# Other places for the steps of an iteration in a chunked RWKV-7 recurrence, and the turned blocks fetched first

## The chip, the cores and the metric
The kernel runs on one core of a Trainium2 chip. The metric is the device time of one execution in microseconds; of the kernel before, three executions were timed. Profiles are taken from one further execution each. TensorE does matmuls, VectorE and ScalarE elementwise work, GpSimd some elementwise work, and SyncE issues the transfers (DMAs) between DRAM and the on-chip memory SBUF. TensorE writes to PSUM, which VectorE and ScalarE read.

## The reference
One layer of a diffusion backbone on 512 latent and 256 context tokens of width 1024: a half-step SwiGLU, then a mixer with two branches (RWKV-7 and RG-LRU, both scanned forwards and backwards, the latent scans starting from the final context states), then another SwiGLU. The change lies in the RWKV-7 scan, for 16 heads of size 64 and both directions:

```
def rwkv_step(s, inp):
    r, w, k, v, kk, kka = inp
    sa = einsum('bhvk,bhk->bhv', s, -kk)
    s = s * w[:, :, None, :] + sa[..., None] * kka[:, :, None, :] + v[..., None] * k[:, :, None, :]
    y = einsum('bhvk,bhk->bhv', s, r)
    return s, y
...
ys, finals = [], []
for d in (forward, backward):
    y, s_fin = rwkv_scan(r, w[d], k[d], v, kk, kk * a[d], s0[d], reverse=d == 1)
```

## The kernel before
The token axis is cut into 12 chunks of 64 tokens (4 of context, 8 latent), and inside a chunk the scan becomes matrix products. A **unit** is a pair of heads in one direction, so there are 16 units (0 to 15; even ones forwards, odd ones backwards). For each unit the kernel does, in this order:

- `loads`: brings features `bk` (b and k), `ar` (a and r) and decays `pc` from DRAM.
- `gram`: products of a and r with b (three operations: context, two halves of the latent chunks) and with k (two). ScalarE copies or VectorE masks them into the tile `gm` (lines 775, 776, 790, 791 and 793). PSUM buffers for these and other side products are called `wk`; there are three of them.
- `out`: the products with b go to DRAM (`nd`, four transfers, line 806) and come back in another layout (`wl`, two, line 810).
- `invert`: VectorE inverts 48 triangular blocks of 32 x 32 (two for each chunk and head) by 31 steps of a multiply (line 826) and a subtraction (line 828) on the tile `yl`. At the end (`end`) GpSimd copies the result turned into `ylt` (line 836), and both go to DRAM as `yd` (line 838) and `yt` (line 840), two transfers each.
- `back`: SyncE fetches the inverses as diagonal blocks into the tile `ybd` (Y in the code, four transfers, line 850), and the turned ones into `y1` (two, line 853). The profile drops the last digit of names, so it prints `y1` as `y`; `y<-yt` is the transfer into y1.
- `merge`: two rounds of 48 small matmuls build the off-diagonal blocks: the first reads `y1` (line 866), the second `ybd` (line 880). ScalarE copies each round's result.
- `fetch`: the decay matrices `dg` (GpSimd, line 897), and turned keys and values.
- `chain`: the serial part, 12 chunks of four steps each (`right`, `solve`, `step`, and reads of the output). ScalarE copies what each gives to the next.
- `finish`: for a pair of units, normalisation, in four operations (`load`, `mean`, `var`, `scale`); it runs in every second iteration.

Besides, a filler puts products of the other branch (tiles `fl`, `fx`, `fraw`) between the chain's steps, where TensorE would wait for ScalarE.

An **iteration** is 24 steps (12 chunks of half a chain) long. In iteration i the chains of units i and i+1 run side by side, four steps a chunk, and the other work belongs to units further ahead: `gram` and the start of `invert` to unit i+3, the end of `invert`, `back` and `merge` to unit i+2. A written table, WIN, says at which step of an iteration each operation stands; the numbers above 24 reach into the next iteration. All operations are sorted by these numbers, and each engine, SyncE's transfers too, gets its instructions in exactly this order, without any rearranging. Units 0 and 1 are inverted in a prologue beside other work. Iteration -1 is the first, with one chain only; iteration 13 is the first without `gram`.

```
                    put(i, zip(WIN["gram"], ops))
                    put(i, [(WIN["out"], out)])
                    put(i, [(WIN["inv"][0] - 0.5, unit_invert(i + 3, WIN["back"], WIN["inv"]))])
                ...
                    put(i, zip(WIN["mrg"], merge(i + 2)))
```

The operations of an inversion (a beginning, 31 steps, `end`) are spread evenly over the stretch WIN["inv"].

Of the kernel before, what the change touches and what calls it, by code (L numbers as in the profile page):

```python
# [8 lines left out]
F32 = mybir.dt.float32  # L9
# [18 lines left out]
NCH = NT // C  # L28
# [28 lines left out]
def hybrid_layer_kernel(ctx: ExitStack, tc, xT, vecs, cst_in, w_mod, wg1, wu1, wd1, w_in, w_up, a_up, g_up,  # L57
                        w_prw, lru_wa, lru_wx, w_plru, w_out, wg2, wu2, wd2, out):
    nc = tc.nc
# [641 lines left out]
    def rwkv_phase(outer, dense_in):  # L701
        with ExitStack() as st:
            open_psum(st, "ps_rwkv")
            units = ExitStack()
            up = units.enter_context(tc.tile_pool(name="units", bufs=1, reuse_waits="tile"))
# [47 lines left out]
            def each_head(out, lhsT, rhs, start=True, stop=True):  # L753

                for h in range(2):
                    PE.matmul(out[hp[h]], lhsT=lhsT[hp[h]], rhs=rhs[hp[h]], start=start, stop=stop)  # L756
# [57 lines left out]
            def invert(i):  # L814
                u = us[i]

                def begin():
                    u["yl"] = up.tile([96, 16, 32], F32, tag="yl", name="yl", bufs=2)
                    V.tensor_copy(u["yl"].rearrange("p i t -> p (i t)"), eye[:96])

                def step(t):
                    def go():
                        yl, wl = u["yl"], u["wl"]
                        ni, nt = t // 2 + 1, 31 - t
                        pr = up.tile([96, 16, 32], F32, tag="pr", name="pr", bufs=1)
                        V.tensor_tensor(out=pr[:, :ni, :nt], in0=yl[:, :ni, t:t + 1].to_broadcast([96, ni, nt]),  # L826
                                        in1=wl[:, t:t + 1, t + 1:].to_broadcast([96, ni, nt]), op=ALU.mult)
                        V.tensor_tensor(out=yl[:, :ni, t + 1:], in0=yl[:, :ni, t + 1:], in1=pr[:, :ni, :nt], op=ALU.subtract)  # L828
                    return go

                def end():
                    yl = u["yl"]
                    yd = dram.tile([48, 32, 32], F32, tag="yd", name="yd", bufs=3)
                    yt = dram.tile([24, 32, 2, 16], F32, tag="yt", name="yt", bufs=3)
                    ylt = up.tile([96, 32, 16], F32, tag="ylt", name="ylt", bufs=1)
                    G.tensor_copy(ylt, yl.rearrange("p i t -> p t i"))
                    for q in range(2):
                        nc.sync.dma_start(out=yd.rearrange("m (i q) t -> m i q t", q=2)[:, :, q, :], in_=yl[48 * q:48 * q + 48])
                    for q in range(2):
                        nc.sync.dma_start(out=yt[:, :, q, :], in_=ylt[48 * q:48 * q + 24])  # L840
                    u["yd"], u["yt"] = yd, yt

                def back():
                    yd, yt = u["yd"], u["yt"]
                    Y = u["Y"] = ybd[i % 3]
                    for b in range(2):
                        for h in range(2):
                            p0 = 64 * h + 32 * b
                            m0 = 24 * b + 12 * h
                            nc.sync.dma_start(out=Y[p0:p0 + 32, :, 32 * b:32 * b + 32], in_=yd[m0:m0 + 12].rearrange("m s t -> s m t"))  # L850
                    u["y1"] = up.tile([128, NCH, 32], F32, tag="y1", name="y1", bufs=1)
                    for h in range(2):
                        nc.sync.dma_start(out=u["y1"][64 * h:64 * h + 32],
                                          in_=yt[12 * h:12 * h + 12].rearrange("m t q i -> t m (q i)"))
                return [begin] + [step(t) for t in range(31)] + [end], back

            def merge(i):
                u = us[i]

                def first():  # L860
                    acc = work()
                    u["mid"] = up.tile([128, NCH * 32], F32, tag="mid", name="mid", bufs=1)
                    for c in range(NCH):
                        for h in range(2):
                            lo, hi = 64 * h, 64 * h + 32
                            PE.matmul(acc[hi:hi + 32, 32 * c:32 * c + 32], lhsT=u["n"][lo:lo + 32, c, 32:64],  # L866
                                      rhs=u["y1"][lo:lo + 32, c, :].rearrange("p (q i) -> p i q", q=2),
                                      start=True, stop=True, tile_position=(lo, hi))
                    for h in range(2):
                        hi = 64 * h + 32  # L870
                        S.activation(u["mid"][hi:hi + 32, :], acc[hi:hi + 32, :NCH * 32], AF.Copy)

                def second():
                    Y = u["Y"]
                    m3 = u["mid"].rearrange("p (c s) -> p c s", s=32)
                    acc = work()
                    for c in range(NCH):
                        for h in range(2):
                            lo, hi = 64 * h, 64 * h + 32
                            PE.matmul(acc[lo:lo + 32, 32 * c:32 * c + 32], lhsT=m3[hi:hi + 32, c, :],  # L880
                                      rhs=Y[hi:hi + 32, c, 32:64], start=True, stop=True, tile_position=(hi, lo))
                    for h in range(2):
                        lo = 64 * h
                        S.activation(Y[lo:lo + 32, :, 32:64],
                                     acc[lo:lo + 32, :NCH * 32].rearrange("p (c s) -> p c s", s=32), AF.Copy)

                return [first, second]
# [35 lines left out]
            def chain(i):  # L923
# [8 lines left out]
                def copied(src, tag):  # L932
                    t = up.tile([128, C], F32, tag=f"{tag}{d}", name=tag, bufs=2)
                    S.activation(t, src, AF.Copy)
                    return t
# [24 lines left out]
                def solve(pos):  # L960
                    def go():
                        c = seq[pos]
                        acc = u["chb"][:, 2 * C:3 * C]
                        each_head(acc, u["Y"][:, c], u["w"])
                        u["u"] = copied(acc, "u")
# [180 lines left out]
            def put(i, ops):  # L1146

                for a, op in ops:
                    at = HOPS * i + a

                    def go(at=at, op=op):
                        with tc.high_priority(tc.cur_priority - base - int(100 * (at + 3 * HOPS))):
                            op()
                    serial[0] += 1
                    todo.append((at, serial[0], go))
# [13 lines left out]
            def unit_invert(i, at, window):  # L1169
                def go():  # L1170
                    ops, back = invert(i)
                    put(i - 3, spread(ops, *window))
                    put(i - 3, [(at, back)])
                return go

            def iteration(i):
# [3 lines left out]
                if i >= 1 and i % 2 == 0:  # L1180
                    put(i, zip(WIN["fin"], finish(i // 2 - 1)))
                if 0 <= i + 4 < NU:
                    put(i, [(9.1, op) for op in loads(i + 4)])
                if 1 < i + 3 < NU:
                    ops, out = gram(i + 3)
# [3 lines that stand above are left out]
                if 1 < i + 2 < NU:  # L1189
                    put(i, zip(WIN["mrg"], merge(i + 2)))  # L1190
                if 0 < i + 2 < NU:
                    put(i, zip(WIN["tm"], fetch(i + 2)))
                if i < NU:
# [9 lines left out]
            def prologue():  # L1203
# [45 lines left out]
                for op in fetch(0):  # L1249
                    op()  # L1250


            WIN = dict(fin=(0.6, 4.6, 8.6, 16.6), gram=(0.7, 3.4, 4.7, 16.7, 20.7), out=5.0, inv=(11.0, 32.0), back=34.0,
                       mrg=(19.4, 22.0), tm=(0.3, 7.4, 8.7, 11.4, 12.7, 15.4), fill=(2.0, 10.0, 18.0), more=(2.0, 6.0, 10.0, 14.0, 18.0, 22.0))
            ALL = {mybir.EngineType.PE, mybir.EngineType.DVE, mybir.EngineType.Activation, mybir.EngineType.Pool, mybir.EngineType.SP}
            PREF = 50000
            SHARE = [6] * 14 + [16] * 3
# [1 line left out]
            with tc.manual_schedule(engines=ALL):  # L1259
                prologue()  # L1260
                fill = filler()
                for i in range(-1, NU):
                    iteration(i)
            with tc.manual_schedule(engines={mybir.EngineType.PE}):
                units.close()
                m = merge_phase(outer)
# [123 lines left out]
    with ExitStack() as outer:  # L1390
        dense_in = outer.enter_context(ExitStack())
        open_hn(dense_in, NT, "right")
        wpool = dense_in.enter_context(tc.tile_pool(name="weights", bufs=1, reuse_waits="tile", side="right"))
        WB = (3, 6, 6)
        ffn1_phase()
        input_phase()
        rwkv_phase(outer, dense_in)
# [67 lines left out]
```

## Time and profile before
| | us |
|---|---|
| median of three executions | 2440.74 |
| lowest and highest | 2434.94 and 2446.79 |
| the profiled execution | 2444.58 |
| its span, from the first to the last instruction | 2442.8 |
| TensorE busy | 2165.1 (89% of the span) |
| VectorE busy | 1320.9 (54%) |
| ScalarE busy | 928.9 (38%) |
| GpSimd busy | 326.0 (13%) |

Outside of the span lie 1.8 us. The recurrence takes the stretch from about 1345 to 1915 us of the span. The busy shares are means over very different stages, so they say nothing of what a place in the recurrence waits for; that is read from the chain of waits and from the order of times on each engine.

### The profile page before, as it was taken

Reading aid. Unit: us, or ns where it says so; the run is one execution under the profiler, and the core shown is the slowest. Engines: PE = TensorE matmul, PEld = TensorE weight load, DVE = VectorE, ACT = ScalarE, POOL = GpSimd, SP = SyncE. Lnnn points to the kernel's source line nnn. Section 1 sums busy time; section 2 is a strip of 40 time slices with the busy share of each in tenths; the row PEclk is TensorE's granted clock in tenths of the full one; section 3 lists DMA queues with packets and bytes.
Section 4 is the critical chain, followed back from the end, with each engine's and each line's share of the span. In section 5 each row is a group of like instructions: output and inputs, shape, how many; then the busy total and the mean of one; then the engine's idle time right before and its main releaser. Section 6 shows DMA issues by size and latency. Waiting matters only on the chain.

```text
span 2442.8 us, 49727 instructions
## 1 busy us (share of the span) xinstructions
PE 2165.1 (89%) x20408; PEld 1826.9 (75%) x20416; DVE 1320.9 (54%) x2795; ACT 928.9 (38%) x1977; POOL 326.0 (13%) x272
## 2 busy tenths in 40 slices
PE   5999999999697988969889788888888698999997
PEld 3788878788685767757667777787787478888886
DVE  5333223233876877778746466667672266333335
ACT  5322212213554556546632333334343235222223
POOL 1000000000352434324100111111111001000000
PEclk8999999999898989989999899999899798999999
DMA  7524342222436564564684445544542442333233
GB/s 290 195 58 147 114 160 70 91 65 74 130 97 112 120 105 116 119 85 127 104 220 137 121 111 128 135 98 126 133 109 76 158 155 87 91 103 99 83 95 91
DMA packets 254662, 289.15 MB, mean 118 GB/s; under 512 B 153953, under 2 KB 172641, under 8 KB 250209
## 3 DMA queue, kind: packets, MB, share of 16 engines
q1 hardware_dynamic: 254144, 285.37, 43.8%
q8 instruction: 160, 2.62, 0.5%
q10 hardware_dynamic: 288, 0.59, 0.1%
q14 instruction: 70, 0.57, 0.1%
HBM read 229.96 MB, written 55.93 MB: 117 GB/s over the span
## 4 chain that ended last, share of the span: by engine, by line
PE 36%; DMA 7%; DVE 4%; issue 2%; ACT 2%; SPq 2%; POOL 0%; DVEq 0%; POOLq 0%; ACTq 0%
PE mm L197 6%; PE mm L198 6%; PE mm L199 6%; PE ch L756 5%; PE wk L756 5%; DMA y<-yt 3%; PE y L957 1%; SPq L850 1%; DVE pr L826 1%; DVE yl L828 1%; PE wk L866 1%; PE fl L1089 1%; DMA ga_d<-sh 1%; DMA wraw<-in_w_in_dram 1%; PE wk L880 1%
## 5 line engine op out<-in xcount | busy, mean ns | idle before, releaser
L197 PE MATMUL mm<-hnh,whi 128*128 128x512 f32 (+1 forms) x1768 | 621.7, 353 | 29.3 <-ACT gr L475 22.3
L198 PE MATMUL mm<-hnl,whi 128*128 128x512 f32 (+1 forms) x1768 | 620.4, 351 | 2.5 <-POOL hnl L203 1.7
L199 PE MATMUL mm<-hnh,wlo 128*128 128x512 f32 (+1 forms) x1768 | 616.6, 349 | 0.0
L161 ACT ACTIVATE whi<-wraw 128x512 fp32r<-128x512 f32 (+3 forms) x264 | 193.5, 735 | 583.7 <-PE mm L198 467.4
L197 PEld LDWEIGHTS mm<-hnh,whi 128*128 128x128 f32 x1768 | 340.8, 193 | 90.6 <-issue 40.2
L179 DVE TENSOR_TENSOR wlo<-wraw,whi 128x512 fp32r<-128x512 f32 (+3 forms) x264 | 216.0, 820 | 316.7 <-ACT whi L161 313.3
L198 PEld LDWEIGHTS mm<-hnl,whi 128*128 128x128 f32 x1768 | 341.3, 193 | 53.2 <-issue 7.4
L199 PEld LDWEIGHTS mm<-hnh,wlo 128*128 128x128 f32 x1768 | 341.1, 193 | 42.5
L197 PE MATMUL mm<-hh,whi 128*128 128x256 f32 (+1 forms) x592 | 201.0, 340 | 0.5 <-ACT hh L202 0.5
L198 PE MATMUL mm<-hl,whi 128*128 128x256 f32 (+1 forms) x592 | 200.6, 339 | 0.3 <-DVE hl L203 0.3
L199 PE MATMUL mm<-hh,wlo 128*128 128x256 f32 (+1 forms) x592 | 200.5, 339 | 0.0
L826 DVE TENSOR_TENSOR pr<-yl,wl 96x126 f32<-96x126 f32 (+22 forms) x496 | 145.9, 294 | 46.2 <-DMA wl<-nd 32.4
L319 DVE TENSOR_TENSOR hf<-mm,sl 128x256 f32<-128x256 f32 (+1 forms) x68 | 40.1, 590 | 209.8 <-PE mm L199 207.9
L828 DVE TENSOR_TENSOR yl<-yl,pr 96x126 f32<-96x126 f32 (+22 forms) x496 | 134.3, 271 | 17.1
L179 POOL TENSOR_TENSOR wlo<-wraw,whi 128x512 fp32r<-128x512 f32 x86 | 134.8, 1568 | 6.1
L203 POOL TENSOR_TENSOR hnl<-nt,hnh 128x256 fp32r<-128x256 f32 (+1 forms) x28 | 27.1, 967 | 783.5 <-ACT hnh L202 649.4
L197 PEld LDWEIGHTS mm<-hh,whi 128*128 128x128 f32 x592 | 112.7, 190 | 15.2 <-issue 1.7
L199 PEld LDWEIGHTS mm<-hh,wlo 128*128 128x128 f32 x592 | 112.6, 190 | 15.2 <-issue 2.5
L198 PEld LDWEIGHTS mm<-hl,whi 128*128 128x128 f32 x592 | 112.6, 190 | 14.1 <-issue 0.8
L161 POOL CAST whi<-wraw 128x512 fp32r<-128x512 f32 x86 | 78.2, 910 | 301.3 <-PE mm L198 223.2
L343 DVE SCALAR_TENSOR_TENSOR res<-mm,scl,res 128x256 f32<-128x256 f32 (+1 forms) x112 | 66.9, 597 | 92.5 <-PE mm L199 91.5
L756 PE MATMUL wk<-ar,bk 64*64 64x128 f32 (+1 forms) x1536 | 95.3, 273 | 2.9 <-DMA ar<-ar_d 2.9
(268 smaller groups left out, 3726.2 us busy)
## 6 DMA issues: line engine op xcount, KB each, us to landing
wm<-in_w_mod_dram SPq DMA_DIRECT2D x32, 1024.0 KB, 5.5
wraw<-in_w_in_dram SPq DMA_DIRECT2D x118, 256.0 KB, 5.8
wraw<-in_wd_dram SPq DMA_DIRECT2D x64, 256.0 KB, 2.8
bk_d<-bk SPq DMA_DIRECT2D x16, 768.0 KB, 13.3
bk<-bk_d SPq DMA_DIRECT2D x16, 768.0 KB, 5.8
wraw<-in_wg_dram SPq DMA_DIRECT2D x44, 256.0 KB, 2.7
wraw<-in_wu_dram SPq DMA_DIRECT2D x44, 256.0 KB
wraw<-in_wg_dram SPq DMA_DIRECT2D x22, 512.0 KB
```

What stands on the lines that cost most here:

```text
L161: self.copy = (lambda o, i: eng.tensor_copy(o, i)) if eng else (lambda o, i: S.activation(o, i, AF.Copy))
L179: self.sub.tensor_tensor(out=l[:, :m], in0=raw[:, :m], in1=h[:, :m], op=ALU.subtract)
L197: PE.matmul(acc, lhsT=wh, rhs=xh, start=k == 0, stop=False)
L198: PE.matmul(acc, lhsT=wh, rhs=xl, start=False, stop=False)
L199: cur["pe"] = PE.matmul(acc, lhsT=wl, rhs=xh, start=False, stop=k == n - 1).ins.name
L203: eng.tensor_tensor(out=lo, in0=src, in1=hi, op=ALU.subtract)
L319: V.tensor_tensor(out=hf[:, :n], in0=pu[:, :n], in1=sl[:, :n], op=ALU.mult)
L343: V.scalar_tensor_tensor(out=res[:, m, q:q + n], in0=acc[:, :n], scalar=scl[:, gi, m, v:v + 1], in1=res[:, m, q:q + n], op0=ALU.mult, op1= ...
L756: PE.matmul(out[hp[h]], lhsT=lhsT[hp[h]], rhs=rhs[hp[h]], start=start, stop=stop)
L826: V.tensor_tensor(out=pr[:, :ni, :nt], in0=yl[:, :ni, t:t + 1].to_broadcast([96, ni, nt]), in1=wl[:, t:t + 1, t + 1:].to_broadcast([96, ni ...
L828: V.tensor_tensor(out=yl[:, :ni, t + 1:], in0=yl[:, :ni, t + 1:], in1=pr[:, :ni, :nt], op=ALU.subtract)
L850: nc.sync.dma_start(out=Y[p0:p0 + 32, :, 32 * b:32 * b + 32], in_=yd[m0:m0 + 12].rearrange("m s t -> s m t"))
```

## The change
Two things change in `invert`, and the table gets other numbers.

- `end`: yd and yt of each half are issued in turn (yd, yt, yd, yt) instead of both yd and then both yt. Both transfers wait for what they read: yd for `yl`, yt for the turned copy.
- `back`: y1 is fetched before `ybd`, and of `ybd` the blocks b = 1, which the second merge reads, first.
- The table: the products with b move from steps 0.7, 3.4, 4.7 to 0.7, 2.0, 3.4; `out` from 5.0 to 3.6; the inversion from 11.0 to 32.0 to 9.5 to 28.0; `back` from 34.0 to 29.5; `merge` from 19.4 and 22.0 to 22.1 and 23.4; the second product with k from 20.7 to 19.4; the filler's first place from 2.0 to 6.0.

```
                     for q in range(2):
                         nc.sync.dma_start(out=yd.rearrange("m (i q) t -> m i q t", q=2)[:, :, q, :], in_=yl[48 * q:48 * q + 48])
-                    for q in range(2):
                         nc.sync.dma_start(out=yt[:, :, q, :], in_=ylt[48 * q:48 * q + 24])
...
                 def back():
                     yd, yt = u["yd"], u["yt"]
+                    u["y1"] = up.tile([128, NCH, 32], F32, tag="y1", name="y1", bufs=1)
+                    for h in range(2):
+                        nc.sync.dma_start(out=u["y1"][64 * h:64 * h + 32],
+                                          in_=yt[12 * h:12 * h + 12].rearrange("m t q i -> t m (q i)"))
                     Y = u["Y"] = ybd[i % 3]
-                    for b in range(2):
+                    for b in (1, 0):
                         for h in range(2):
...
-            WIN = dict(fin=(0.6, 4.6, 8.6, 16.6), gram=(0.7, 3.4, 4.7, 16.7, 20.7), out=5.0, inv=(11.0, 32.0), back=34.0,
-                       mrg=(19.4, 22.0), ...
+            WIN = dict(fin=(0.6, 4.7, 8.6, 16.6), gram=(0.7, 2.0, 3.4, 16.7, 19.4), out=3.6, inv=(9.5, 28.0), back=29.5,
+                       mrg=(22.1, 23.4), ...
```

The order of SyncE's transfers in one iteration with `finish`, before (y_14775 is y1 of this unit, ybd_10268 its Y):

```order
L895 DMA vs<-zv_d 128x768
L1097 DMA plru_d<-sg 128x256
L806 DMA nd<-gm 32x12x32 x4
L810 DMA wl<-nd 48x1024 x2
L838 DMA yd<-yl 768x1x32 x2
L840 DMA yt<-ylt 768x1x16 x2
L1018 DMA fa<-ga_d 128x512
L1019 DMA fa<-gb_d 128x512
L741 DMA bk<-bk_d 128x1536
L743 DMA ar<-ar_d 128x1280
L747 DMA pc<-pc_d 128x12
L850 DMA ybd_10268<-yd 32x12x32 x4
L853 DMA y_14775<-yt 32x12x32 x2
```

The same place in the changed kernel:

```order
L895 DMA vs<-zv_d 128x768
L838 DMA yd<-yl 768x1x32
L839 DMA yt<-ylt 768x1x16
L838 DMA yd<-yl 768x1x32
L839 DMA yt<-ylt 768x1x16
L806 DMA nd<-gm 32x12x32 x4
L810 DMA wl<-nd 48x1024 x2
L846 DMA y_14660<-yt 32x12x32 x2
L853 DMA ybd_10268<-yd 32x12x32 x4
L1097 DMA plru_d<-sg 128x256
L1018 DMA fa<-ga_d 128x512
L1019 DMA fa<-gb_d 128x512
```

yd and yt, which belong to the unit before, now stand ahead of nd and wl, and y1 stands right behind wl.

VectorE at the end of an inversion (of the changed kernel; the last two operations of a step of `yl` end in a shape of 96x16, and L819 begins the next inversion):

```order
L828 TENSOR_TENSOR yl<-yl,pr 96x14x5
L776 TENSOR_TENSOR gm<-wk,cst 128x256
L826 TENSOR_TENSOR pr<-yl,wl 96x14x4
L828 TENSOR_TENSOR yl<-yl,pr 96x14x4
L826 TENSOR_TENSOR pr<-yl,wl 96x15x3
L828 TENSOR_TENSOR yl<-yl,pr 96x15x3
L791 TENSOR_TENSOR gm<-wk,cst 128x256
L826 TENSOR_TENSOR pr<-yl,wl 96x15x2
L828 TENSOR_TENSOR yl<-yl,pr 96x15x2
L826 TENSOR_TENSOR pr<-yl,wl 96x16
L828 TENSOR_TENSOR yl<-yl,pr 96x16
L791 TENSOR_TENSOR gm<-wk,cst 128x256
```

Before, all three masks of the products with b stood inside the inversion (L776 after the step of shape 96x11x11, the last L791 after that of 96x14x5); now the last one stands behind it.

SyncE at the start of iteration -1, as a difference (fraw and fr are the filler's first loads):

```order
 L895 DMA vs<-zvr_d 128x768
+L806 DMA nd<-gm 32x12x32 x4
+L810 DMA wl<-nd 48x1024 x2
 L1049 DMA fraw<-in_w_plru_dram 128x512
 L1060 DMA fr<-ylru_d 128x256 x4
```

nd and wl of unit 2 stand ahead of these loads now; before, they stood behind them and eight more.

## Rows read from the trace of the kernel before
**Rows 1.** Chain of waits, 1580 to 1622 us: start, length, what.
```profile
1580.01 4.36 DMA y<-yt
...
1616.88 4.91 DMA y<-yt
```
**Rows 2.** Waits, 1412 to 1861 us: in total, times, longest.
```profile
PE wk L866 <- DMA y<-yt: 45.2, 12, 5.4
```
**Rows 3.** Stretches: length, busy PE, PEld, DVE, ACT, POOL, granted clock, DMA share, GB/s.
```profile
1584.40:1590.10 5.70, 5.69 (x106) 5.47 (x106) 2.31 (x8) 1.36 (x5) 0.00 (x0) 0.50 0.50 156
1592.70:1617.10 24.40, 23.24 (x558) 21.22 (x560) 17.74 (x64) 10.35 (x40) 2.90 (x3) 1.00 0.43 105
1617.40:1621.90 4.50, 0.00 (x0) 0.01 (x1) 4.16 (x13) 0.15 (x1) 0.80 (x1) 0.98 0.85 126
```
**Rows 4.** Timeline of SyncE, one iteration: start, time of issuing, transfer.
```profile
1600.73 1.86 SPq L806 DMA_DIRECT2D nd<-gm  x4
1605.41 0.78 SPq L810 DMA_DIRECT2D wl<-nd  x2
1606.29 1.31 SPq L838 DMA_DIRECT2D yd<-yl  x2
1607.64 2.59 SPq L840 DMA_DIRECT2D yt<-ylt  x2
...
1612.91 3.92 SPq L850 DMA_DIRECT2D ybd<-yd  x4
1616.88 3.29 SPq L853 DMA_DIRECT2D y<-yt  x2
```
**Rows 5.** Timeline of VectorE, the same iteration; in brackets its wait before.
```profile
1602.69 0.19 DVE L828 TENSOR_TENSOR yl<-yl,pr 96x16 f32<-96x16 f32 x1
...
1609.17 0.19 DVE L826 TENSOR_TENSOR pr<-yl,wl 96x31 f32<-96x31 f32 x1 [0.82 <-DMA wl<-nd]
...
1615.76 0.69 DVE L1029 TENSOR_TENSOR fa<-fa 128x512 f32<-128x512 f32 x1 [0.20 <-DMA fa<-gb_d]
...
1616.97 1.36 DVE L826 TENSOR_TENSOR pr<-yl,wl 96x115 f32<-96x115 f32 x1
```
**Rows 6.** Timeline of GpSimd, the same iteration.
```profile
1603.00 1.06 POOL L836 COPY ylt<-yl 96x512 f32<-96x512 f32 x1 [19.78 <-issue]
...
1616.73 1.47 POOL L897 TENSOR_TENSOR dg<-eye,pc 128x768 f32<-128x768 f32 x1 [8.66 <-PE ch L756]
```
**Rows 7.** Groups of VectorE, 1412.8 to 1794.5 us: busy, mean | idle before.
```profile
L826 DVE TENSOR_TENSOR pr<-yl,wl 96x126 f32<-96x126 f32 (+22 forms) x339 | 101.8, 300 | 34.4 <-DMA wl<-nd 25.1
L828 DVE TENSOR_TENSOR yl<-yl,pr 96x126 f32<-96x126 f32 (+22 forms) x340 | 93.1, 274 | 11.7
L793 DVE TENSOR_TENSOR gm<-wk,cst 128x512 f32<-128x512 f32 x22 | 15.2, 689 | 46.7 <-PE wk L756 46.7
L791 DVE TENSOR_TENSOR gm<-wk,cst 128x256 f32<-128x256 f32 x22 | 9.2, 418 | 5.5 <-ACT gm L790 5.5
```
**Rows 8.** Timeline of VectorE: the last subtraction of inversions 2 and 15.
```profile
1396.81 0.18 DVE L828 TENSOR_TENSOR yl<-yl,pr 96x16 f32<-96x16 f32 x1
...
1843.10 0.19 DVE L828 TENSOR_TENSOR yl<-yl,pr 96x16 f32<-96x16 f32 x1
```
**Rows 9.** Timeline of SyncE behind inversion 15, with nothing queued ahead.
```profile
1846.05 1.66 SPq L840 DMA_DIRECT2D yt<-ylt  x2
```
**Rows 10.** Timelines of SyncE and VectorE in iteration -1 (unit 2).
```profile
1352.65 0.42 SPq L1049 DMA_DIRECT2D fraw<-in_w_plru_dram  x1
...
1364.11 1.86 SPq L806 DMA_DIRECT2D nd<-gm  x4
1367.39 0.78 SPq L810 DMA_DIRECT2D wl<-nd  x2
...
1371.01 0.19 DVE L826 TENSOR_TENSOR pr<-yl,wl 96x31 f32<-96x31 f32 x1 [2.13 <-DMA wl<-nd]
```
**Rows 11.** Timeline of TensorE in iteration 13.
```profile
1842.58 0.58 PE L1089 MATMUL fl<-fx,fhi 128*128 128x256 f32 x1 [5.62 <-DVE sg L1096]
```

More of the change, by code (lines that the diff above doesn't have):

```diff
@@ L850, in back @@
                             nc.sync.dma_start(out=Y[p0:p0 + 32, :, 32 * b:32 * b + 32], in_=yd[m0:m0 + 12].rearrange("m s t -> s m t"))
[L851 to L854, printed above, removed]
                 return [begin] + [step(t) for t in range(31)] + [end], back
@@ L1250, in prologue @@
                     op()
-            WIN = dict(fin=(0.6, 4.6, 8.6, 16.6), gram=(0.7, 3.4, 4.7, 16.7, 20.7), out=5.0, inv=(11.0, 32.0), back=34.0,
-                       mrg=(19.4, 22.0), tm=(0.3, 7.4, 8.7, 11.4, 12.7, 15.4), fill=(2.0, 10.0, 18.0), more=(2.0, 6.0, 10.0, 14.0, 18.0, 22.0))
+            WIN = dict(fin=(0.6, 4.7, 8.6, 16.6), gram=(0.7, 2.0, 3.4, 16.7, 19.4), out=3.6, inv=(9.5, 28.0), back=29.5,
+                       mrg=(22.1, 23.4), tm=(0.3, 7.4, 8.7, 11.4, 12.7, 15.4), fill=(6.0, 10.0, 18.0), more=(2.0, 6.0, 10.0, 14.0, 18.0, 22.0))
             ALL = {mybir.EngineType.PE, mybir.EngineType.DVE, mybir.EngineType.Activation, mybir.EngineType.Pool, mybir.EngineType.SP}
```

## The prediction
> **What bounds the kernel now.** I read the chain of waits first. In the recurrence (about 1345 to 1915 us of the span) its longest piece in nearly every iteration is the transfer of the turned inverse, y1 (the profile prints it as y<-yt), into SBUF: [rows 1] show two, of 4.36 and 4.91 us. The list of waits counts twelve stops of TensorE for it before the matmuls of line 866, 45.2 us, 3.8 each [rows 2]. The table by stretches shows what else a stop costs: after it come 5.7 us at a granted clock of 0.50, the lower level of 1.2 GHz, where the undisturbed stretch has 1.00 [rows 3]. At half clock 5.7 us do the work of 2.85, so a stop costs 6.6 us in the mean.
>
> Next I asked why y1 is late. Its issue on SyncE stands last in a line: nd, wl, yd, yt, the loads of the iteration, four ybd, y1 [rows 4]. From nd at 1600.73 to the start of y1 are 16.15 us, and it lands 4.9 us later [rows 1]. The inverse itself was ready long before: its last subtraction ends at 1602.88 and its turned copy at 1604.06, but yd is issued at 1606.29, when wl ahead of it has got the landing of nd [rows 4 to 6]. So **SyncE issues in order, and a transfer that waits holds all behind it**. The ring that sets an iteration is: Gram products with b, nd, wl, ..., y1, merge, next Gram products. The inversion on VectorE is not in it; VectorE waits for wl (0.82 us at 1609.17 [rows 5]). From the end of inversion 2 to that of inversion 15 are 446.3 us, 34.3 for each of 13 [rows 8].
>
> **What the change removes.** y1 is issued before ybd, and all of `back` 4.5 steps earlier, while the merge stands 2.7 steps later. In the new order on SyncE y1 follows wl directly, so it lands about 6 us after wl's issue (its issues and 4.9 us), and at the merge TensorE has been served for long. The stop of [rows 1] goes: by themselves twelve stops of 6.6 us are 79 us.
>
> **What it puts in its place.** The end of the inversion moves from step 7.4 to 3.4 of an iteration, and the out-transfer only from 5.0 to 3.6: on SyncE yd and yt of unit u now stand *before* nd of unit u+1. nd(u+1) waits behind yt(u), which waits for the end of inversion u; inversion u+1 waits for wl(u+1). That is a new ring, on VectorE and SyncE, and I cost it from the end E of one inversion to the start S of the next.
>
> The turned copy on GpSimd starts 0.12 after E and takes 1.06 [rows 5, 6]: 1.18.
>
> Then yt, yd, yt: the first yd (0.65) goes beside the copy. yd is 1.31 for two [rows 4], yt 1.66 for two where nothing is queued ahead, 2.59 where wl is [rows 4, 9]. Now nothing big is ahead, so 0.83 + 0.65 + 0.83 and 0.15 of small gaps: 2.45.
>
> From nd's first issue to wl's are 3.28 us in one unit, 4.68 in another [rows 4, 10]; nd now goes behind the 768 small pieces of each yd and yt, so I take 4.45.
>
> From wl's issue to the first multiply are 3.62 and 3.76 [rows 4, 5, 10]: 3.6.
>
> The sum is 11.7 us; from the same rows it can be 10.5 (with 3.28 for nd) or 13.2 (with yt at 1.3 each and 0.5 more for nd).
>
> S to E: the steps take 101.8 + 93.1 us in 11 inversions, 17.7 each, with (34.4 - 25.1) + 11.7 us of small gaps, 1.9 each [rows 7]. By the new order two masks of L793 (0.69) and two of 256 columns (0.42, L791 and L776 alike) stand inside: 2.2. In the trace each inversion meets two GpSimd operations and is slowed: a multiply of 0.27 takes 1.36 beside `dg` [rows 5, 6]. `dg` stays inside; one of the weight splits, because the fill moved to step 6, falls every other time into the 11.7 us in which VectorE waits anyhow: -0.5. Together 21.3. Inversions 5, 7, ..., 15 also hold three operations of `scale` (0.69 each [rows 5]): 23.4.
>
> So **an iteration costs 33.0 or 35.1 us by the new ring**, against 34.3 in the trace. 13 x 33.0 + 6 x 2.1 = 441.6; two splits more in inversion 11 (+1.0), no context masks in 15 (-0.8): 441.8, which is 4.5 less than 446.3.
>
> **What of it is hidden.** The other moved parts cost nothing as long as TensorE has slack, and it has: an iteration with `finish` took 1584.4 to 1621.9 = 37.5 us, less 4.5 of stop and 2.85 of slow clock [rows 3] 30.1; one without has less work; the ring has 68.1 us for a pair. TensorE will now wait at step 4.7 or 7.4, for a PSUM buffer of the three of `wk` that VectorE's mask, queued behind inversion steps, has not read. Behind that matmul stand the next steps of both chains; nobody on the ring waits for them. The merge at 22.1 and 23.4 leaves the copies of the second merge 1.9 steps (some 2 us) until the first solve; a delay there would be TensorE's, not the ring's. The order b = 1 first in ybd, and the pairing of yd and yt, only matter for y1 and are free.
>
> **The two ends.** In the first iteration nd now precedes the filler's first loads on SyncE; before, these stood first (1352.65 against nd at 1364.11 [rows 10]). nd comes about 5 us earlier (at 1359, when its products are ready without the filler's work between), but the loads, behind wl, only 4 us after that, at 1363, some 10 us later than before, and VectorE's order has five splits of the filler's operand (fx) ahead of the first step. From 1363 by the same distances I estimate the start of inversion 2 at 1376, 5 us later, and its end, which before had waits for TensorE in it, 2 us later: bounds -5 and +7. At the other end, TensorE waits 5.6 us for a VectorE operation inside inversion 15 [rows 11]; this wait, just behind E of unit 15, stays, so nothing more is won there.
>
> **Sum**: -4.5 + 2 = -2.5 us against the profiled 2444.58, which is 3.84 above the median of the three runs: **2438 us**.
>
> **A rule that speaks against the change.** By the rows yd stood 3.4 us ready at SyncE, from 1602.88 to 1606.29 [rows 4, 5]. The Trainium skill, "DMA: Bandwidth & Descriptors", section "Anatomy of one DMA — SWDGE (gpsimd) path", says that the DMA engines wait for no semaphore: every wait is on the issuing sequencer before dispatch. By that rule, with which the trace agrees, nd cannot pass yt.
>
> **Rivals.**
>
> **The stop goes and nothing comes in its place** (nd not held, or held for a short time). For it: the wait is large and plainly of y1. Against: the ring above needs 33 us where TensorE needs 30. It would give 2441 - 79 = 2362. Chance 0.04.
>
> **The hand-over is faster**: nd lands as in the quick unit (3.28), and GpSimd's operations fall into VectorE's wait: 10.5 and a mean of 21.6 for the inversion, 32.1 an iteration; 13 x (34.3 - 32.1) = 29, less 2 for the start: 2414. Half of it, 2428, is as likely; from about 1.1 us an iteration it is faster by 0.5%. Chance 0.23.
>
> **The hand-over is slower**: yd and yt are 768 pieces each, in one line with nd; if yt takes 1.3 each as in [rows 4] and nd lands behind them, E to S is 13.2, 1.5 more an iteration. It decides from 1.2 us an iteration. 13 x 1.5 = 19.5: 2458, on the other side. With it `gb`, for which VectorE already waits 0.20 us in `scale` [rows 5] and which now stands behind y1 and ybd, could be late inside six inversions; 1 us each makes 2464. Chance 0.19.
>
> **The change does what it says, and the rings are worth the same** (my forecast): 0.54.
>
> **How the numbers follow.** 0.5% is 12.2 us, about what a measurement of this kernel can tell from no change. Faster: 0.04 + 0.23 = 0.27. Same: 0.54. Slower: 0.19. The forecast's own range, with 10.9 to 12.5 us for the hand-over and the bounds of the start, is 2428 to 2450. For 8 in 10 I reach to 2418 (most of the faster hand-over) and 2461 (most of the slower one).
>
> **What would show it.** No stop of L866 for y<-yt, but TensorE idle some 4 us at step 4.7 or 7.4 for VectorE; on SyncE yd and yt directly after the last subtraction, and nd some 3.7 us after it; first multiply 11 to 12.5 us after the last subtraction, released by wl, in nearly every iteration; inversions of 21 to 24 us instead of 28 to 30. It is wrong if nd is issued before yt, if VectorE's first step is not released by wl, or if inversions take much longer than 23.4, waiting for TensorE or for gb.

## The result and the profile after

The changed kernel takes 2464.18 us in the median of four runs (2459.47 to 2466.10), against 2441.08 before; the ratio measured is 1.0092 (95% interval 1.0064 to 1.0121). It is slower, by 20 us or more, and outside of both ranges that the prediction gave (2428 to 2450, and 2418 to 2461). A second set of runs, f0_again below, gave 1.0089 (1.0064 to 1.0114). The profiled execution after took 2459.47 us, the fastest of its four runs, with a span of 2457.6.

The chain of waits shows whether the ring changed. Each row gives the shares of one stretch of the recurrence by engine and line; the first is of the kernel before (1412 to 1843 us), the second of the changed one (1412 to 1849 us).

```profile
by line: PE wk L756 23.7%; PE ch L756 22.7%; DMA y<-yt 14.3%; PE y L957 5.5%; SPq L850 5.2%; PE wk L866 4.3%; PE wk L880 3.2%; issue 2.8%; ACT ybd L884 2.7%; PE fl L1089 2.6%; DVE pr L826 1.8%; DVE yl L828 1.6%; PE wk L1003 1.5%; PE wk L101
```
```profile
by line: DVE pr L826 20.6%; DVE yl L828 20.4%; DMA wl<-nd 10.0%; PE wk L756 8.7%; DMA nd<-gm 7.1%; PE ch L756 5.9%; issue 5.6%; SPq L806 3.8%; DVE gm L793 3.6%; DVE gm L791 1.1%; SPq L839 1.1%; SPq L810 1.0%; DVE fa L1027 1.0%; DVE fa L1029
```

Before, the chain ran over TensorE and the transfer of y1. Now it runs over the inversion's two operations, nd and wl; y1 is gone from it. The list of waits of the changed kernel, 1412 to 1861 us (in total, times, longest), answers to [rows 2]:

```profile
DVE pr L826 <- DMA wl<-nd: 79.9, 13, 13.7
...
PE wk L756 <- DVE gm L793: 16.2, 11, 2.5
...
PE wk L866 <- DVE fa L1026: 3.8, 5, 1.5
```

L866 no longer waits for y1. VectorE waits for wl before each of the thirteen inversions, 79.9 us in all. One hand-over, on SyncE (start, time of issuing), GpSimd and VectorE, answers to [rows 4 to 6]:

```profile
1606.92 0.60 SPq L838 DMA_DIRECT2D yd<-yl  x1
1608.14 0.82 SPq L839 DMA_DIRECT2D yt<-ylt  x1
1609.01 0.59 SPq L838 DMA_DIRECT2D yd<-yl  x1
1609.65 0.79 SPq L839 DMA_DIRECT2D yt<-ylt  x1
1610.49 2.99 SPq L806 DMA_DIRECT2D nd<-gm  x4
1615.03 1.36 SPq L810 DMA_DIRECT2D wl<-nd  x2
1616.50 0.87 SPq L846 DMA_DIRECT2D y<-yt  x2
```
```profile
1607.02 1.10 POOL L836 COPY ylt<-yl 96x512 f32<-96x512 f32 x1 [12.75 <-issue]
```
```profile
1606.71 0.18 DVE L828 TENSOR_TENSOR yl<-yl,pr 96x16 f32<-96x16 f32 x1
1606.82 0.41 DVE L791 TENSOR_TENSOR gm<-wk,cst 128x256 f32<-128x256 f32 x1
...
1619.06 0.19 DVE L826 TENSOR_TENSOR pr<-yl,wl 96x31 f32<-96x31 f32 x1 [2.87 <-DMA wl<-nd]
```

From the end of the last subtraction (1606.89) to the next inversion's first multiply (1619.06) are 12.17 us. nd's last input, the mask of L791, is there at 1607.23, yet nd is issued at 1610.49, behind the last yt.

To place the 20 us I cut the span at marks that all kernels have: the ends of inversions 0, 1, 2 and 15 (E0, E1, E2, E15; the last subtraction of `yl`) and the start of the chain's last copy (L). The marks of the changed kernel, on VectorE and ScalarE:

```profile
1303.14 0.19 DVE L828 TENSOR_TENSOR yl<-yl,pr 96x16 f32<-96x16 f32 x1
...
1338.75 0.19 DVE L828 TENSOR_TENSOR yl<-yl,pr 96x16 f32<-96x16 f32 x1
...
1405.04 0.18 DVE L828 TENSOR_TENSOR yl<-yl,pr 96x16 f32<-96x16 f32 x1
...
1849.23 0.18 DVE L828 TENSOR_TENSOR yl<-yl,pr 96x16 f32<-96x16 f32 x1
```
```profile
1923.64 0.23 ACT L934 ACTIVATE u<-ch 128x64 f32<-128x64 f32 x1 [0.49 <-PE ch L756]
```

The same marks were read in every profile. Times are us; the ratio is to the runs of the kernel before on the same chip, with its interval. The last column is the mean hand-over, from the end of inversions 2 to 14 to the first multiply of the next.

| kernel | median, ratio | to E0 | E0-E1 | E1-E2 | E2-E15 | E15-L | L-end | hand-over |
|---|---|---|---|---|---|---|---|---|
| before | 2441.08 | 1301.0 | 32.5 | 63.5 | 446.3 | 67.8 | 531.7 | 5.8 |
| before, g0_before | (one run: 2442.44) | 1299.0 | 33.0 | 63.7 | 445.4 | 68.3 | 531.3 | 5.8 |
| changed | 2464.18, 1.0092 (1.0064-1.0121) | 1303.3 | 35.6 | 66.3 | 444.2 | 74.2 | 534.0 | 12.4 |
| f0_again | 2458.44, 1.0089 (1.0064-1.0114) | 1304.1 | 35.7 | 66.1 | 440.6 | 73.8 | 535.1 | 12.1 |
| e1_fetch | 2425.66, 0.9951 (0.9932-0.9970) | 1296.6 | 36.2 | 63.9 | 427.8 | 68.6 | 532.3 | 5.6 |
| e2_table | 2444.60, 1.0022 (1.0007-1.0037) | 1299.0 | 32.8 | 66.1 | 436.5 | 70.8 | 538.7 | 11.8 |
| e3_nd_first | 2413.38, 0.9902 (0.9880-0.9923) | 1301.6 | 36.0 | 67.1 | 394.6 | 73.6 | 533.1 | 7.0 |
| e4_edges | 2453.05, 1.0062 (1.0040-1.0084) | 1299.9 | 35.4 | 66.8 | 442.9 | 68.8 | 538.7 | 12.3 |
| f1_pairs | 2450.55, 1.0057 (1.0038-1.0076) | 1297.3 | 35.6 | 67.0 | 434.9 | 73.9 | 536.5 | 11.7 |
| f3_ends | 2411.81, 0.9903 (0.9877-0.9930) | 1299.9 | 34.9 | 68.0 | 398.0 | 68.0 | 537.7 | 7.0 |
| f4_back | 2397.02, 0.9843 (0.9815-0.9870) | 1300.5 | 35.5 | 67.5 | 387.4 | 68.1 | 534.2 | 7.0 |
| g1_start | 2393.99, 0.9811 (0.9786-0.9836) | 1298.4 | 33.9 | 63.4 | 393.4 | 67.9 | 535.2 | 7.5 |
| h1_tie | 2462.30, 1.0088 (1.0068-1.0109) | 1304.2 | 36.6 | 66.6 | 444.0 | 74.2 | 532.3 | 12.4 |
| h2_all | 2388.60, 0.9784 (0.9764-0.9805) | 1303.6 | 33.1 | 62.5 | 390.8 | 66.0 | 531.4 | 7.1 |

Two executions of one kernel differ by up to 3.6 us in the iterations (444.2 and 440.6), by 2.0 us to E0, by 1.1 us behind L and by half a microsecond or less in the three short stretches. In the means of two profiles each, the change costs 2.9 us in the prologue (E0-E1), 2.6 at the start (E1-E2), gives 3.5 back over the iterations, and costs 6.0 behind the last inversion and 3.1 behind the recurrence. The iterations went about as forecast; what these marks can place of the loss lies at their ends.

### The profile page after: what moved, and what is told of

It is laid out like the page before. It is cut to its first block, busy times and chain, and to the rows that moved or that the text cites. A ratio compares the mean times of both kernels' runs of the same rounds, so it can differ in the third digit from the quotient of the medians.

```text
span 2457.6 us, 49767 instructions
## 1 busy us (share of the span) xinstructions
PE 2182.7 (89%) x20416; PEld 1839.0 (75%) x20416; DVE 1317.4 (54%) x2795; ACT 933.3 (38%) x1977; POOL 326.8 (13%) x272
## 4 chain that ended last, share of the span: by engine, by line
PE 27%; DVE 13%; DMA 7%; issue 3%; SPq 2%; ACT 2%; POOL 0%; DVEq 0%; POOLq 0%; ACTq 0%
PE mm L198 6%; PE mm L197 6%; PE mm L199 6%; DVE pr L826 4%; DVE yl L828 4%; PE wk L756 3%; PE ch L756 2%; DMA wl<-nd 2%; DMA nd<-gm 1%; DMA ar_d<-ar 1%; SPq L806 1%; DVE gm L793 1%; DMA wraw<-in_w_prw_dram 1%; PE ch L197 1%; PE ch L198 1%
## 5 line engine op out<-in xcount | busy, mean ns | idle before, releaser
L826 DVE TENSOR_TENSOR pr<-yl,wl 96x126 f32<-96x126 f32 (+22 forms) x496 | 136.1, 274 | 94.2 <-DMA wl<-nd 79.9
L756 PE MATMUL wk<-ar,bk 64*64 64x128 f32 (+1 forms) x1536 | 104.9, 297 | 20.0 <-DVE gm L793 16.2
```

## The experiments

**Is it the table or the code?** e1_fetch takes the code of the changed kernel with the table of before, e2_table the reverse.

```
-            WIN = dict(fin=(0.6, 4.7, 8.6, 16.6), gram=(0.7, 2.0, 3.4, 16.7, 19.4), out=3.6, inv=(9.5, 28.0), back=29.5,
+            WIN = dict(fin=(0.6, 4.6, 8.6, 16.6), gram=(0.7, 3.4, 4.7, 16.7, 20.7), out=5.0, inv=(11.0, 32.0), back=34.0,
...
```

> The two edits of code (yd and yt in turn; y1 ahead of ybd) with the table of before. Theory A (the ring of before ends in y1, and the loss of the change lies in its ends, the prologue and the last iterations): y1 is issued 3.97 us earlier in each iteration, so TensorE's stops at L866 shrink from 45.2 us to under 15, and 12 iterations get some 3 to 4 us shorter; in the prologue the weights of the gates still wait behind y1 (+3.1). 2441 - 12 x 3.5 + 3 = about 2402. Rival B (the place of y1 in the fetch is worth nothing, since the wait goes over to ybd and L880): stops of 3 us at L880 take the place of those at L866, and the time is 2441 to 2446.

Measured: 0.9951, half a per cent faster. Neither theory had it: the iterations win 18 us, not 42, and the prologue loses 3.7. The list of waits, 1412 to 1843 us, the chain's shares of the same stretch, and two of its pieces show where the rest went:

```profile
PE wk L866 <- DMA y<-yt: 34.2, 13, 5.5
```
```profile
by line: PE wk L756 17.3%; DMA y<-yt 17.2%; PE ch L756 16.7%; issue 7.6%; DMA yt<-ylt 4.6%; PE y L957 4.3%; PE wk L866 3.5%; PE wk L880 2.5%; ACT ybd L884 2.5%; PE fl L1089 2.3%; DMA nd<-gm 1.9%; DVE pr L826 1.8%; DVE yl L828 1.6%; SPq L838
```
```profile
1569.65 6.85 DMA y<-yt
...
1603.97 7.83 DMA y<-yt
```

y1 is issued earlier, but from its issue to its landing now pass 6.85 and 7.83 us where [rows 1] have 4.36 and 4.91; in the chain's twelve pieces each the mean is 6.7 us against 5.1. The chain also waits for the landing of yt, which y1 reads (4.6% of the stretch). So most of the head start is lost. The loads issued just ahead of y1 are likely what stretches it: in these two stretches the DMA engines move 207 and 245 GB/s, against 105 and 152 in those of [rows 1]. No run takes the loads away, so this cause is not shown.

> The new table alone, with yd, yd, yt, yt and ybd ahead of y1 as before. Theory A: the same ring as in the changed kernel (end of an inversion to the first multiply of the next 12.4 us), y1 comes 4 us later but lands long before the merge at step 22.1; the prologue loses 3.1 us less. About 2461. Rival B (the fetch order is what the new table needs): TensorE stops at L866 for y1 in every iteration, 2480 or more.

Measured: 2444.60, 1.0022. The table alone costs next to nothing, so the expectation of 2461 failed and so did the rival. Rows of the stretches: the hand-over is 11.8 us instead of 12.4, the iterations take 436.5, the prologue has its old 32.8, and E15-L is 70.8 instead of 74. In the new table the two edits of code are the greater part of the loss, though in the old one they win half a per cent.

**Is the new ring what an iteration costs?** e3_nd_first puts the products with b and the out-transfer so early that SyncE issues nd and wl ahead of yd and yt again.

```
-            WIN = dict(... gram=(0.7, 2.0, 3.4, 16.7, 19.4), out=3.6, ...
+            WIN = dict(... gram=(0.3, 1.0, 1.7, 16.7, 19.4), out=1.9, ...
```

> The changed kernel with the products with b at 0.3, 1.0 and 1.7 and the out-transfer at 1.9, so that on SyncE nd and wl of unit u+1 stand ahead of yd and yt of unit u again. Theory A (the new ring, end of inversion, copy, yd and yt, nd, wl, next inversion, is what an iteration costs): the first multiply comes 4 to 7 us behind the end of the inversion before, not 12.4, and iterations fall from 34.2 to about 30, TensorE's own time: 2464 - 13 x 4.2 = about 2410. Rival B (the iteration is held by TensorE's waits for VectorE's masks, or by TensorE itself, not by this ring): within 8 us of 2464.

Measured: 2413.38, 0.9902. The hand-over falls to 7.0 us in the mean (from about 3 to 10) and an iteration from 34.2 to 30.4 (394.6 / 13). That is theory A, to 4 us. SyncE of this kernel at one hand-over, and the chain, 1412 to 1799 us:

```profile
1643.98 2.98 SPq L806 DMA_DIRECT2D nd<-gm  x4
1648.42 0.78 SPq L810 DMA_DIRECT2D wl<-nd  x2
1649.30 0.61 SPq L838 DMA_DIRECT2D yd<-yl  x1
```
```profile
by line: PE wk L756 20.2%; PE ch L756 19.2%; issue 5.8%; DVE yl L828 5.0%; DVE pr L826 4.8%; PE y L957 4.2%; DMA fraw<-in_w_plru_dram 3.2%; DMA fa<-ga_d 2.8%; PE wk L866 2.5%; PE wk L880 2.4%; SPq L853 2.4%; PE fl L1089 2.4%; ACT mid L871 2
```

TensorE leads the chain again, and y1 is not in it: neither ring sets the iteration any more. The granted clock tells the same: 0.92 in the iterations before, 0.90 in the changed kernel, 0.97 here, so the change alone gave TensorE no clock back.

**The ends.** e4_edges fetches ybd ahead of y1 for units 0 and 1, and leaves unit 15 at its old places.

```
-                    put(i, [(WIN["inv"][0] - 0.5, unit_invert(i + 3, WIN["back"], WIN["inv"]))])
+                    early = i + 3 < NU - 1
+                    put(i, [(WIN["inv"][0] - 0.5, unit_invert(i + 3, WIN["back"] if early else 34.0, WIN["inv"] if early else (11.0, 32.0)))])
...
+                    for op in (blocks, turned) if i < 2 else (turned, blocks):
```

> The changed kernel with the two ends as before: for units 0 and 1 ybd is fetched ahead of y1, and unit 15 keeps the old places of its inversion (11.0 to 32.0) and of its fetch (34.0). Theory A (3.1 us are lost in the prologue and 6 us behind the last inversion): the profile loses both, 2464 - 9 = about 2455. Rival B (the time between the medians lies in the iterations, or comes from the clock behind the recurrence): within 3 us of 2464.

Measured: 2453.05, 1.0062, theory A's time, though only one of its two gains came. The tail is shown: E15-L falls from 74 to 68.8. The prologue is not: it stays at 35.4. With e2_table at 32.8 and f1_pairs at 35.6, either edit alone, y1 ahead or yd and yt in turn, costs the whole 3 us there. SyncE of the changed kernel behind the last inversion, ScalarE of the changed kernel, then SyncE and ScalarE of e4_edges, show what the tail loses:

```profile
1852.14 0.80 SPq L839 DMA_DIRECT2D yt<-ylt  x1
1854.85 0.84 SPq L846 DMA_DIRECT2D y<-yt  x2
1855.80 2.91 SPq L853 DMA_DIRECT2D ybd<-yd  x4
...
1859.27 0.43 SPq L1049 DMA_DIRECT2D fraw<-in_w_plru_dram  x1
```
```profile
1862.06 0.63 ACT L202 ACTIVATE fhi<-fraw 128x512 fp32r<-128x512 f32 x1 [4.40 <-DMA fraw<-in_w_plru_dram]
```
```profile
1844.78 0.38 SPq L1055 DMA_DIRECT2D fraw<-in_w_plru_dram  x1
...
1846.46 0.60 SPq L838 DMA_DIRECT2D yd<-yl  x1
```
```profile
1852.65 0.63 ACT L202 ACTIVATE fhi<-fraw 128x512 fp32r<-128x512 f32 x1 [0.54 <-PE fl L1096]
```

y1 waits at SyncE for the landing of yt (1.9 us) and holds the filler's load; issuing y1 and ybd ahead of it takes 3.9 us more. ScalarE waits 4.40 us for that load, and the chain's next copies, which stand behind it on ScalarE, wait with it. With unit 15 at its old places the load is out before yd.

In the prologue it is the load of the gates' weights (`wraw`) that waits. SyncE before, then of the changed kernel, and ScalarE of each, which copies the load's high part (`whi`) for VectorE:

```profile
1302.60 1.72 SPq L840 DMA_DIRECT2D yt<-ylt  x2
1304.61 1.89 SPq L850 DMA_DIRECT2D ybd<-yd  x4
1306.60 0.92 SPq L853 DMA_DIRECT2D y<-yt  x2
1307.56 0.94 SPq L1111 DMA_DIRECT2D wraw<-in_w_in_dram  x2
```
```profile
1306.55 0.80 SPq L839 DMA_DIRECT2D yt<-ylt  x1
1309.22 0.86 SPq L846 DMA_DIRECT2D y<-yt  x2
1310.20 1.93 SPq L853 DMA_DIRECT2D ybd<-yd  x4
1312.18 0.94 SPq L1111 DMA_DIRECT2D wraw<-in_w_in_dram  x2
```
```profile
1310.89 1.31 ACT L202 ACTIVATE whi<-wraw 128x512 fp32r<-128x512 f32 x2 [7.22 <-DMA wraw<-in_w_in_dram]
```
```profile
1316.15 1.29 ACT L202 ACTIVATE whi<-wraw 128x512 fp32r<-128x512 f32 x2 [10.17 <-DMA wraw<-in_w_in_dram]
```

From E0 (1300.96 and 1303.33) to `wraw` are 6.60 us before and 8.85 after. Inside inversion 1 VectorE waits for these splits of `wraw` 7.7 us before, 10.8 after, 10.6 in e4_edges and 10.9 in f1_pairs, but 7.8 in e2_table: these are the 3 us.

**The pairs.** f0_again is the changed kernel, run beside f1_pairs, which issues yd, yd, yt, yt as before.

```
                     for q in range(2):
                         nc.sync.dma_start(out=yd.rearrange("m (i q) t -> m i q t", q=2)[:, :, q, :], in_=yl[48 * q:48 * q + 48])
+                    for q in range(2):
                         nc.sync.dma_start(out=yt[:, :, q, :], in_=ylt[48 * q:48 * q + 24])
```

> The changed kernel itself, on the same chip as the three others. Theory A (its loss sits in the two ends and in the pairing of yd and yt, all inside of the recurrence): the stretches from E0 to E1, from E1 to E2 and from E15 to the last step of the chain again take some 35.6, 66 and 74 us, and the time is 2460 to 2466. Rival B (the ends differ from execution to execution): at least one of these three is within 2 us of the kernel before (32.5, 63.5, 67.8).

> The changed kernel with yd, yd, yt, yt in place of yd, yt, yd, yt. Theory A (a yd between the two yt stands in the ring, 0.57 us an iteration, and some 2 us in the prologue): the hand-over falls from 12.4 to 11.8 us, and the time is 2464 - 13 x 0.57 - 2 = about 2454.5. Rival B (the pairing is free, as the prediction had it): 2461 to 2467, and the 20 us between the changed kernel and the table alone come from the place of y1.

Measured: 2458.44 and 2450.55, 8 us apart, with intervals that overlap a little; the ends of the changed kernel repeat (35.7, 66.1, 73.8). The hand-over is 11.7 against 12.1 and 12.4 us, the iterations 434.9 against 440.6 and 444.2. That is theory A: both yd fit beside the turned copy, and the second one, put between the two yt, takes its 0.60 us from the ring. The 2 us expected in the prologue are not there, since y1 still stands first.

**Building on it.** f3_ends is e3_nd_first with the pairs undone and unit 15 at its old places; f4_back has the fetch at 33.0 in addition.

```
-            WIN = dict(... out=1.9, inv=(9.5, 28.0), back=29.5,
+            WIN = dict(... out=1.9, inv=(9.5, 28.0), back=33.0,
```

> The kernel with nd and wl ahead of yd and yt (2413), and the pairs undone, and unit 15 at its old places. Theory A (prologue 3 us, tail 5 us, both apart from the ring): about 2405. Rival B (with the ring broken these no longer matter, since other waits take their place): 2410 to 2416.

> As the last one, with the fetch of y1 and ybd at 33.0 in place of 29.5, so that y1's wait on SyncE for the landing of yt holds no loads. Theory A (TensorE's own work is the bound, and what is left are loads behind y1, in the chain of waits some 4 us an iteration in every second one): 2385 to 2400. Rival B (TensorE alone is the bound): within 4 us of the last kernel.

Measured: 2411.81, which by time is rival B of the first. The tail falls by 5.6 us as A had it, but the prologue only by 1.1, since y1 still stands first there, the iterations take 3.4 more, about as much as executions of one kernel differ, and the stage behind 4.6 more, where kernels with the same order of work differ as much (see below). f4_back takes 2397.02, 15 us less, and 29.8 us an iteration (387.4 / 13), with y1's wait behind the loads. Of the chain over its iterations some seven tenths are now TensorE's work; VectorE's inversion has 10% and issue 5%.

g0_before is a second profile of the kernel before. g1_start has the prologue of before and the filler's first loads ahead of nd in iteration -1.

```
-                put(i, zip(WIN["fill"] if n < 9 else WIN["more"], lumps(fill[:n], 3 if n < 9 else 6)))
+                put(i, zip(((0.1, 10.0, 18.0) if i < 0 else WIN["fill"]) if n < 9 else WIN["more"], lumps(fill[:n], 3 if n < 9 else 6)))
```

> The kernel before once more, for a second profile, since its first profiled execution (2444.58) was 6 to 7 us above the medians of its later runs (2438). Theory A (the stretches named so far are all that differs): its stretches in the prologue, the start, the iterations and behind the last inversion are within 2 us of the first profile's (32.5, 63.5, 446.3, 67.8), and what is faster lies outside of them. Rival B (the first profile had a slow recurrence): the iterations take 440 us or less.

> The last kernel (fetch at 33.0, 2397) with units 0 and 1 as before (yd, yd, yt, yt, then ybd, then y1) and with the filler's first loads at 0.1 in iteration -1, so ahead of nd again. Theory A (the prologue loses 3 us by y1's place there, the start 3 us by the loads' place behind wl): E0 to E1 falls from 35.5 to 32.6, E1 to E2 from 67.5 to 64, and the time to about 2391. Rival B (the start is late for its masks and steps, not for the loads): E1 to E2 stays above 66 and the time within 3 us of 2394.

Measured: the profile before repeats to 1 us in every stretch behind E0. In g1_start the start goes back to 63.4 and the prologue to 33.9, as theory A had it (64 and 32.6); 6 us more in the iterations leave 3 us of the gain (2393.99).

**A third end.** L-end is 531.3 to 532.3 in the three profiles with the old table and 533.1 to 538.7 in the nine with the new one. The order on TensorE there differs: `fin` 4.7 shares its step with the second column of the merge stage, and of two operations at one step the one put first goes first. Twenty-one matmuls of that column now come ahead of the mean of the last `finish` (L1003, L1011). h1_tie is the changed kernel without that tie, h2_all is g1_start without it.

```
-                put(NU, zip((0.5, 4.7, 8.7, 16.7), early([("ch0", 1), ("ch1", 1), ("fl", 1), ("y", 2)])))
+                put(NU, zip((0.5, 4.75, 8.75, 16.7), early([("ch0", 1), ("ch1", 1), ("fl", 1), ("y", 2)])))
```

> The changed kernel with the four columns of the merge stage that come behind the recurrence at 0.5, 4.75, 8.75, 16.7 in place of 0.5, 4.7, 8.7, 16.7. With the second operation of finish moved from 4.6 to 4.7 these shared a step, and 21 matmuls of the second column came ahead of the mean of the last finish. Theory A (that order is a third place at which the change loses time): from the last step of the chain to the end of the span are 531 to 532.5 us as in the two profiles of before, not 534 to 535, and the time falls by 3 us. Rival B (these 3 us are chance, as the other differences outside of the recurrence): 534 us or more, and no fall.

> The kernel with nd first, the fetch at 33.0, the ends as before and the filler's loads first (2394), with the columns behind the recurrence at 4.75 and 8.75 as well. Theory A: another 3 us, about 2391, and 531 to 532.5 us behind the last step of the chain. Rival B: within 2 us of 2394, and 535 us there.

Measured: L-end falls to 532.3 and 531.4, as in the kernel before. The time of h1_tie (1.0088) does not fall with it; 3 us lie within the intervals, so the third end is shown in the profiles alone; h2_all is at 2388.60, 5 us below g1_start, and at 0.9784 the fastest version. TensorE before, then of the changed kernel:

```profile
1940.84 1.87 PE L1003 MATMUL wk<-fa,cst 128*128 128x512 f32 x2
...
1947.42 0.95 PE L1011 MATMUL wk<-cst,fa 128*128 128x2 f32 x8
```
```profile
1958.65 1.02 PE L1003 MATMUL wk<-fa,cst 128*128 128x512 f32 x2
1961.11 1.20 PE L1011 MATMUL wk<-cst,fa 128*128 128x2 f32 x8 [1.45 <-ACT fa L1006]
```

Counted from L (1911.12 and 1923.64) the mean starts at 29.7 before and at 35.0 after. The matmuls that used to cover its way through VectorE and ScalarE are already used up: TensorE waits 1.45 us for L1006. In h1_tie the mean starts at 30.1 again.

## Why the prediction was wrong

**The stop of y1** went, as forecast.

**The new ring** came as the prediction costed it. In the changed kernel's first profile the terms measured, as means of thirteen hand-overs, are 1.24 for the copy (forecast 1.18), 2.35 for yt, yd, yt (2.45), 0.09 to nd, 4.6 from nd to wl (4.45) and 4.1 to the first multiply (3.6). With that the hand-over is 12.4, inside the stated 10.5 to 13.2. Inversions take 21.1 us in the mean without `scale` and 22.6 with it (21.3 and 23.4). E2 to E15 came to 444.2 and 440.6 us; the forecast was 441.8. That it came so close is in part luck: in the first profile the hand-overs took 9 us more than forecast and the inversions nearly 7 less. e3_nd_first, which breaks the ring and nothing else of size, wins 46 to 50 us in this stretch, so the ring is shown. The 30.4 and 29.8 us an iteration of e3_nd_first and f4_back stand close to the 30.1 that the prediction took for TensorE in an iteration with `finish`; that TensorE alone sets them is not shown. The Trainium skill, "DMA: Bandwidth & Descriptors", section "Anatomy of one DMA — SWDGE (gpsimd) path", says that waits sit on the issuing sequencer; the trace agrees, here for transfers issued from SyncE, for nd's input stood ready from 1607.23 until nd's turn at 1610.49.

**TensorE's new wait** for VectorE's mask is there, but 1.5 us each (16.2 us in eleven), not 4.

**The step that failed is "The two ends".** At the first, +2 was forecast and 2.6 measured, and g1_start, where the filler's first loads and work stand ahead of nd again, puts it on their place behind wl. But the prologue, where units 0 and 1 go through the same `end` and `back` with weights queued behind, had no term at all: 2.9 us. At the other end the prediction said that the wait behind E of unit 15 "stays, so nothing more is won there", and did not ask what would be lost: 6.0 us, since y1, four steps earlier, now waits ahead of the filler's load (with the table alone 2.7 of these are lost, by e2_table). Behind the recurrence `fin` 4.7, a number that the list of changes does not name, ran into the next stage's table for another 3.1. These three terms, which the sum put at nothing, are 12 us, and with them the stated -2.5 becomes about +9.5.

**"Free" was wrong for the pairing too.** "The order b = 1 first in ybd, and the pairing of yd and yt, only matter for y1 and are free": the pairing costs 0.4 to 0.65 us of each hand-over, and in the prologue either it or y1 ahead of ybd costs 3 us. In the sum the second yd was counted (0.65), which is why the iterations still came out; its cost was not seen as a choice of the change.

**The slower rival** had the sign and, by chance, the time (2458 to 2464), not the cause. The iterations did not get longer than before.

**What stays open.** The six stretches differ by 14.8 us between the means of two profiles each, of which the ends and the iterations hold 11.1. The other 3.7 lie ahead of E0, where the change touches no instruction. The changed kernel has 1303.3 and 1304.1 there and its variant h1_tie 1304.2, but f1_pairs has 1297.3 with the same instructions, so no cause can be named. The medians are 20 to 23 us apart. The profiled executions of before (2444.58 and 2442.44) stand above or at the upper end of the medians of its runs (2437.50 to 2442.68), the first of the changed kernel below all its other runs, and what the unprofiled runs do otherwise is not known.

## What to carry to other kernels

When a step is moved in a repeated order, walk the first and the last passes through the new order too, and the stage that follows: there the same few instructions stand before other neighbours, and a transfer that waits at the head of an in-order queue holds a load that nobody held before. A transfer moved ahead does not land earlier by the same time if others now run beside it. And a wait that is removed is only worth what lies between it and the next ring: here the stop was put at 79 us, and removing it won 3.5 in the iterations, because the ring that replaced it cost about the same. With nd ahead of yd and yt as well the iterations won 51 us, and 58 in f4_back, less than the 79.

## What the hardware showed

The time from y1's issue to its landing depends on its place: twelve pieces of the chain take 4.4 to 6.4 us before, and 4.7 to 9.4 in e1_fetch, where y1 goes ahead of ybd and right behind the loads. What stretches it was not isolated.

Issuing on SyncE has no fixed price either. The two transfers of y1 take 0.92 us to issue at 1306.60, behind ybd alone, and 3.29 in [rows 4], behind the loads and ybd. In most places yd takes 0.59 to 0.65 us and yt 0.79 to 0.83.
